# Seven of 22 K-tile pairs of a down projection as Strassen's seven block products

## The chip, the cores and the metric

The kernel runs on one core of one Trainium2 chip. The metric is the device time of one execution in microseconds, from the first to the last instruction and what the launch puts around them; it is given as a median of a few runs. The engines that matter here are TensorE (PE, the matrix multiplier), VectorE (DVE), ScalarE (ACT) and SyncE (SP), whose queue issues the DMAs. Each engine works through its own instructions in the order in which the program lists them and waits on semaphores for the others.

## The reference

One decoder layer on 256 tokens of width 2048, in float32: an input projection, two attention branches that are merged, an output projection, a layer norm, a gated MLP, a second layer norm and a per-layer embedding. The change lies in the MLP and what follows it:

```python
def conv_gated_mlp(x, w_gate, w_up, conv_w, conv_b, w_down):
    g = causal_dwconv(x @ w_gate, conv_w, conv_b)
    h = jax.nn.gelu(g) * (x @ w_up)       # (256, 5632)
    return h @ w_down                     # (256, 5632) @ (5632, 2048)
...
ffn = conv_gated_mlp(x, ...)
x = layer_norm(ALPHA * x + ffn, ln2_g[i], ln2_b[i])
x = x + jax.nn.sigmoid(x @ w_ple_gate[i]) * (p[i] @ w_ple_proj[i])
```

## The kernel before, in words

**Three products for one.** Every operand of a matmul is split into a rounded part `hi` (a ScalarE copy to the type float32r) and a rest `lo` (a VectorE subtraction `raw - hi`). A product is summed from three: hi·hi, hi·lo and lo·hi.

**Units of weights.** All large weights lie in one DRAM array `wu` of units of 128 x 2048 floats (1 MB). `unit()` hands out the next unit and first lets `prep()` (L93) prepare units until two beyond it are under way. For each half of a unit `prep()` issues a DMA into a `raw` buffer (SP, L99), the ScalarE copy to `hi` (L77, in the helper `copy`) and the VectorE subtraction to `lo` (L103). There are four `raw` buffers and six buffers each for `hi` and `lo`, of 128 x 1024 floats; they are reused in rotation, so a new `hi` waits until the matmuls have read the one six places before it.

**Gate and up projection.** For each of 44 tiles `n` of the hidden width (128 channels) the kernel multiplies one unit of `w_gate` and one of `w_up` with all 256 tokens (`gate_up`, L169 and L171), adds the parts (`comb`), applies convolution and GELU, and multiplies. The product `y` (128 channels x 256 tokens) is split into `hi` and `lo` and kept in the list `hT`, the stationary operand of the next stage. This costs one ScalarE copy (L77, `hT<-yc`) and one VectorE subtraction (L989) for each `n`.

**Down projection.** `residual("dn", ...)` calls `x_half` (L227) twice, once for each half `nh` of the 2048 output columns. Each half has four PSUM banks (two token blocks `t` of 128, two column blocks `c` of 512) and goes through 22 units. A unit holds two K tiles of 128 channels by 1024 columns, and costs 24 matmuls of 128x128 by 512 columns (`x_mm`, L213): two K tiles, two token blocks, three products, two column blocks. After the last unit of a half the four banks are added to the residual `z` (L813) and layer norm statistics are taken (L814). In the second half the last two units are kept for a tail which finishes one bank after the other, so that the second layer norm (`ln_out`), its transposes and the projections that follow begin while TensorE still multiplies.

**Order and memory.** The Tile scheduler orders the instructions of TensorE, ScalarE and VectorE, by the program order and by priorities where they are given; the order of SP's DMAs is that of the program. The pool `big` (`s8`) has 15 buffers of 128 x 2048 floats. Activations, residuals and the layer norm's gains share them. PSUM has eight banks: six in the pool `pmm` (`mmtile`) and two in `pmx` (`mxtile`), both used in rotation. In the first half of the down projection, after its unit 4, `mid2` issues the loads of the residual (`z<-x1d`, 2 x 1 MB) and of the gains (`lnb`, 2 x 1 MB).

Of the kernel before, what the change touches and what calls it, by code (L numbers as in the profile page):

```python
# [9 lines left out]
F32 = mybir.dt.float32  # L10
F32R = mybir.dt.float32r
# [23 lines left out]
P_LN1 = (2000, 2000)  # L35
P_LN2 = (4000, 1000)
ZN_DVE = (0,)
AFF_DVE = (0, 2)
# [8 lines left out]
def tile_block(ctx: ExitStack, tc: tile.TileContext, wu, wfv, wpp, xT_in, x_in, pT_in, wlr,  # L47
# [41 lines left out]

    n_prep = [0]  # L90
    ready = {}

    def prep():  # L93
        u = n_prep[0]
        n_prep[0] += 1
        his, los = [], []
        for h in range(2):
            raw = ring.tile([P, 1024], F32, tag="raw", bufs=4, name=f"raw{u}_{h}")
            nc.sync.dma_start(raw, wu[u, :, h * 1024:(h + 1) * 1024])  # L99
            hi = ring.tile([P, 1024], F32R, tag="hi", name=f"hi{u}_{h}")  # L100
            copy(hi, raw)
            lo = ring.tile([P, 1024], F32R, tag="lo", name=f"lo{u}_{h}")
            nc.vector.tensor_tensor(lo, raw, hi.bitcast(F32), ALU.subtract)  # L103
            his.append(hi)
            los.append(lo)
        ready[u] = (his, los)

    n_used = [0]
    NU = wu.shape[0]

# [609 lines left out]

    def ln_out(zs, stats, t, act_out, cg, cb, nm, prio):

        z = zs[t]
        mv = sm.tile([P, 8], F32, tag="mv", name="mv")
# [5 lines left out]
        with tc.high_priority(prio):  # L730
            for g in range(4):
                zc = z[:, g * 512:g * 512 + 512]
                if g in ZN_DVE:
# [83 lines left out]

    def affine(zs, gb_, after, gs=range(4)):
        for t in range(2):
            for g in gs:  # L820
                zc = zs[t][:, g * 512:g * 512 + 512]
                nc.vector.tensor_tensor(zc, zc, gb_[0][:, g * 512:g * 512 + 512], ALU.mult)
                yield
                nc.vector.tensor_tensor(zc, zc, gb_[1][:, g * 512:g * 512 + 512], ALU.add)
                yield
            after(t)
# [45 lines left out]
    def end1(tail_mm):  # L872
# [3 lines left out]
        with tc.manual_schedule(engines={mybir.EngineType.PE}):  # L876
# [59 lines left out]
            for j in range(4):  # L936
                if j < 3:
# [3 lines left out]

    residual("wo", mT, 16, z1, st1, (mid1, lambda: pq.append(ple_prep(0))), end=end1)
    mixers.append(affine(z1, gain[0], lambda t: nc.gpsimd.dma_start(x1d[t], z1[t]),
                         [g for g in range(4) if g not in AFF_DVE]))

# [5 lines left out]
    for i in range(2):  # L951
        nc.gpsimd.memset(gp[i][:, 0:2], 0.0)
    hT = [None] * 11

    def lt(shape, dt, name):
        return late.tile(shape, dt, name=name)

# [8 lines left out]
    for n in range(NF):  # L966
        if n % 4 == 0:
            hT[n // 4] = (s8 if n < 40 else lt)([P, 4, 512], F32R, name=f"hT{n // 4}")
        psg = gate_up(f"psg{n}")
# [15 lines left out]
        comb(psu, u)  # L985
        nc.vector.tensor_tensor(y, y, u, ALU.mult)
        dst = hT[n // 4][:, n % 4, :]
        copy(dst[:, 0:256], y)
        nc.vector.tensor_tensor(dst[:, 256:512], y, dst[:, 0:256].bitcast(F32), ALU.subtract)  # L989
        if n >= 4:  # L990
            pull(1)

    z2 = [s8([P, 2048], name=f"z2{t}") for t in range(2)]
    st2 = [sm.tile([P, 4, 6], F32, tag=f"st2{t}", bufs=1, name=f"st2{t}") for t in range(2)]

    def mid2():
        for t in range(2):
            nc.sync.dma_start(z2[t], x1d[t])
        gain[1] = load_gain(1)

    x2T = [s8([P, 4, 512], F32R, name=f"x2T{g}") for g in range(4)]
    pb, pq = [], []

    def done2(t):
        if t == 1:
            pb.extend(ple_proj(1, *pq[0]))
        ln_out(z2, st2, t, x2T, c_g2, c_b2, "l2", P_LN2[t])

    residual("dn", hT, NF, z2, st2, (mid2, lambda: pq.append(ple_prep(1))), done2)
    pp = [s8([P, 2, 1024], name=f"ppk{i}") for i in range(2)]  # L1010
    for t in range(2):
        for c in range(2):
            copy(pp[1][:, t, c * 512:c * 512 + 512], pb[t][c][0])
    mixers.append(affine(z2, gain[1], lambda t: None))

# [6 lines left out]
    for nh in range(2):  # L1022
        def ev_o(t, c, ps, ab=(0, 512), nh=nh):
            th = t2("tho")
            r = t2("res")
            e = slice(*ab)
            w = slice(c * 512 + ab[0], c * 512 + ab[1])
            o = slice(nh * 1024 + w.start, nh * 1024 + w.stop)
            nc.scalar.activation(th[:, e], ps, AF.Tanh, bias=0.0, scale=0.5)
            nc.vector.scalar_tensor_tensor(th[:, e], th[:, e], 1.0, pp[nh][:, t, w],  # L1030
                                           ALU.add, ALU.mult)
            nc.vector.scalar_tensor_tensor(r[:, e], th[:, e], 0.5, z2[t][:, o],
                                           ALU.mult, ALU.add)
            nc.sync.dma_start(out[t, :, o], r[:, e])
# [15 lines left out]
def _xst(w):  # L1050

    k, n = w.shape
    a = w.reshape(k // 256, 2, P, n // 1024, 1024).transpose(3, 0, 2, 1, 4)
    return a.reshape((k // 256) * (n // 1024), P, 2048)


# [9 lines left out]
def _layout(i):  # L1066
# [4 lines left out]
    for n in range(16):  # L1071
        br.append(bg[n:n + 1])
        if n % 2 == 0:
# [5 lines left out]
         _wst(c("ma", 2048)), _wst(c("mb", 2048))] + br  # L1079
        + [_xst(i["w_out"][0]), gu, _xst(i["w_down"][0]),  # L1080
           _xst(i["w_ple_gate"][0])], 0)
# [43 lines left out]
```

## Time and profile before

| What | Value |
|---|---|
| Median of 3 runs | 1710.17 us (1709.9 to 1710.96) |
| The profiled execution | 1709.5 us |
| Its span, first to last instruction | 1707.6 us |
| PE busy | 1698.3 us (99%) |
| DVE busy, ACT busy | 1098.6 us (64%), 833.4 us (49%) |
| Down projection on the chain that ended last | PE dn L213, 14% of the span |

The page counts an engine as busy while its instructions run; the duration of a matmul overlaps that of the next, so the time of one matmul in a stream is read from the distance of the starts. Times in the trace count from the start of the span. The down projection begins at 1359.2 us, its second half at 1481.5 us, and the tail's transposes (`ptl`) begin at 1601.97 us.

### The profile page before, as it was taken

How to read it: one execution, taken by the hardware profiler on the slowest of the kernel's cores; microseconds unless marked ns; L12 is line 12 of the kernel's file. 1: busy time of each engine (PE TensorE's matmuls, PEld its weight loads, DVE VectorE, ACT ScalarE, POOL GpSimd, SP SyncE). 2: the span in 40 equal slices, each digit the busy share in tenths (PEclk: the TensorE clock that was granted, in tenths of full speed). 3: DMA queues.
4: the chain of work that ended last, by engine and by line, in shares of the span. 5: the costliest groups of instructions: out<-in, count | busy, mean ns of one | idle time of the engine just before them, and what ended most of it. 6: DMA issues, size and time to landing. Idle time of an engine off the chain costs nothing.

```text
span 1707.6 us, 23836 instructions
## 1 busy us (share of the span) xinstructions
PE 1698.3 (99%) x9035; PEld 1455.7 (85%) x9035; DVE 1098.6 (64%) x1588; ACT 833.4 (49%) x1200; POOL 39.3 (2%) x123
## 2 busy tenths in 40 slices
PE   9999999999999999999999999999999999999998
PEld 8888888888888888888788888888888888888787
DVE  6666668758756557774687666666666644544774
ACT  5745445445555544443365445444544533334633
POOL 0000000000000000000010000000000000000000
PEclk9999999999999999999999999999999999999999
DMA  8654455555554555557665555555555575556444
GB/s 310 231 190 166 163 185 173 181 177 172 179 176 165 173 185 189 192 185 281 207 217 195 189 190 187 191 189 186 187 193 187 186 291 189 183 196 197 157 174 171
DMA packets 91427, 330.22 MB, mean 193 GB/s; under 512 B 10232, under 2 KB 11904, under 8 KB 89904
## 3 DMA queue, kind: packets, MB, share of 16 engines
q1 hardware_dynamic: 90528, 324.51, 56.0%
q0 software_dynamic: 784, 4.20, 0.7%
q8 instruction: 70, 1.15, 0.3%
q14 instruction: 45, 0.37, 0.1%
HBM read 323.42 MB, written 5.25 MB: 192 GB/s over the span
## 4 chain that ended last, share of the span: by engine, by line
PE 97%; DVE 1%; DMA 0%; ACT 0%; SPq 0%; issue 0%; POOL 0%
PE dn L213 14%; PE psu L169 9%; PE psg L169 9%; PE psm L169 7%; PE gr L213 5%; PE gv L213 5%; PE wo L213 5%; PE pg L213 5%; PE psu L171 5%; PE psg L171 5%; PE psm L171 4%; PE psa L169 3%; PE fv L320 2%; PE psa L171 2%; PE psfq L169 2%; PE psq L169 2%
## 5 line engine op out<-in xcount | busy, mean ns | idle before, releaser
L103 DVE TENSOR_TENSOR lo<-raw,hi 128x1024 fp32r<-128x1024 f32 x568 | 694.1, 1224 | 520.6 <-ACT hi L77 519.6
L77 ACT ACTIVATE hi<-raw 128x1024 fp32r<-128x1024 f32 x568 | 601.7, 1060 | 745.8 <-issue 275.9
L169 PE MATMUL psu<-x1T,hi 128*128 128x512 f32 x688 | 242.2, 394 | 0.0
L169 PE MATMUL psg<-x1T,hi 128*128 128x512 f32 x672 | 236.5, 393 | 0.0
L213 PE MATMUL dn<-hi,hT 128*128 128x512 f32 x704 | 193.5, 394 | 0.0
L171 PE MATMUL psu<-x1T,lo 128*128 128x256 f32 x688 | 192.6, 280 | 0.0
L171 PE MATMUL psg<-x1T,lo 128*128 128x256 f32 x672 | 188.1, 280 | 0.0
L169 PE MATMUL psm<-xT,hi 128*128 128x512 f32 x512 | 180.1, 395 | 0.0
L213 PEld LDWEIGHTS dn<-hi,hT 128*128 128x128 f32 x704 | 132.1, 188 | 30.6
L169 PEld LDWEIGHTS psu<-x1T,hi 128*128 128x128 f32 x688 | 129.4, 188 | 29.5
L169 PEld LDWEIGHTS psg<-x1T,hi 128*128 128x128 f32 x672 | 126.4, 188 | 28.9
L171 PE MATMUL psm<-xT,lo 128*128 128x256 f32 x512 | 143.3, 280 | 0.0
L171 PEld LDWEIGHTS psu<-x1T,lo 128*128 128x128 f32 x688 | 129.4, 188 | 0.0
L171 PEld LDWEIGHTS psg<-x1T,lo 128*128 128x128 f32 x672 | 126.4, 188 | 0.0
L169 PEld LDWEIGHTS psm<-xT,hi 128*128 128x128 f32 x512 | 96.2, 188 | 21.6
L213 PE MATMUL dn<-lo,hT 128*128 128x512 f32 x352 | 111.3, 393 | 0.0
L171 PEld LDWEIGHTS psm<-xT,lo 128*128 128x128 f32 x512 | 96.5, 188 | 0.2
L169 PE MATMUL psa<-oT,hi 128*128 128x512 f32 x256 | 90.1, 393 | 0.0
L213 PEld LDWEIGHTS dn<-lo,hT 128*128 128x128 f32 x352 | 66.1, 188 | 15.7
L213 PE MATMUL gv<-hi,xT 128*128 128x512 f32 x256 | 73.6, 399 | 0.0
L213 PE MATMUL gr<-hi,xT 128*128 128x512 f32 x256 | 73.5, 399 | 0.0
L213 PE MATMUL wo<-hi,mT 128*128 128x512 f32 x256 | 71.8, 395 | 0.0
(248 smaller groups left out, 2438.8 us busy)
## 6 DMA issues: line engine op xcount, KB each, us to landing
raw<-in_wu_dram SPq DMA_DIRECT2D x568, 512.0 KB, 3.6
fvraw<-in_wfv_dram SPq DMA_DIRECT2D x14, 524.0 KB, 6.3
lnb<-in_lng_dram SPq DMA_DIRECT2D x4, 1024.0 KB, 12.4
z<-in_x_dram SPq DMA_DIRECT2D x2, 1024.0 KB, 9.6
praw<-in_wpp_dram SPq DMA_DIRECT2D x4, 512.0 KB, 4.8
x1d<-z POOLq DMA_DIRECT2D x2, 1024.0 KB, 4.4
z<-x1d SPq DMA_DIRECT2D x2, 1024.0 KB, 7.6
xraw<-in_xT_dram SPq DMA_DIRECT2D x7, 256.0 KB, 6.5
```

The lines of the kernel that those rows point to most:

```text
L77: nc.scalar.activation(o, i, AF.Copy, bias=0.0, scale=scale)
L103: nc.vector.tensor_tensor(lo, raw, hi.bitcast(F32), ALU.subtract)
L169: nc.tensor.matmul(ps, lhsT=hi[i // 8 if hoff == 0 else 0][:, w0 % 1024:w0 % 1024 + P], rhs=a[:, kt % 4, :], start=first and i == 0, stop= ...
L171: nc.tensor.matmul(ps[:, 256:512], lhsT=lo[i // 8 if hoff == 0 else 0][:, w0 % 1024:w0 % 1024 + P], rhs=a[:, kt % 4, 0:256], start=False, ...
L213: nc.tensor.matmul(bs[j][:, 0:m], lhsT=x, rhs=v[:, o:o + m], start=first and i == 0, stop=last and i == 2)
L320: nc.tensor.matmul(fbk[t][c][:, 0:n], lhsT=x, rhs=w[:, o:o + n], start=kt == 0 and i == 0, stop=kt == 15 and i == 2)
```

## The change

Write a pair of K tiles as a product of 2 x 2 blocks: the activations as blocks of 128 tokens by 128 channels, the weights as blocks of 128 channels by 512 columns. The plain product needs eight block products, Strassen's (in Winograd's form) seven. The three float32r products for each block product stay. Of the 22 pairs, seven (`DN_S`) are multiplied so, in both halves: 21 matmuls for a unit in place of 24.

Left operands: for each of these pairs `sums()` makes four sums and differences of activation blocks (VectorE), and splits seven blocks into `hi` and `lo`. For the pairs 1, 4 and 7 this follows their `n`; for the pairs 10, 13, 16 and 19 (`DN_Y`) `y` is kept unsplit in a buffer `hY`, and `sums()` stands after the loop over `n`.

Right operands: `prep_s()` takes the place of `prep()` for these units, in both halves. It makes four differences T1 to T4 of weight blocks (VectorE) and splits seven blocks in six pieces: b21 and b22 together as one half unit of 1024 columns, and b11 and T1 to T4 one by one, 512 columns each. It takes six `hi` and six `lo` buffers, where a plain unit takes two of each.

The products go to seven PSUM banks: three are banks of the plain result, four (p1, p5, p6, p7) are new and are summed over all seven pairs. After the last such pair `fold()` adds them to the residual `z2` (one ScalarE copy, eight VectorE operations for each half). The plain result is added at the end of the half as before, with an add in place of a multiply-add. The units come in the order `DN_ORDER` (plain C, Strassen S): C S C C S C S C C S C S C C S C S C C C C C. The weights are laid out for this on the host.

Loads: the residual is loaded by halves (2 x 512 KB each), after unit 8 of the first half and after unit 6 of the second; the gains after unit 11 of the second half. The per-layer embedding's preparation (`ple_prep(1)`) stays after unit 17 of the second half.

```diff
+DN_S = (1, 4, 7, 10, 13, 16, 19)
+DN_Y = (10, 13, 16, 19)
+DN_ORDER = (0, 1, 2, 3, 4, 5, 7, 6, 8, 10, 9, 13, 11, 12, 16, 14, 19, 15, 17, 18, 20, 21)
...
+    def split512(src, name):
+        hi = ring.tile([P, 512], F32R, tag="hi", name=f"{name}h")
+        copy(hi, src)
+        lo = ring.tile([P, 512], F32R, tag="lo", name=f"{name}l")
+        nc.vector.tensor_tensor(lo, src, hi.bitcast(F32), ALU.subtract)
+        return hi, lo
+
+    def prep_s(u):
+        r0, r1 = [ring.tile([P, 1024], F32, tag="raw", bufs=4, name=f"raw{u}_{h}")
+                  for h in range(2)]
+        for h, r in enumerate((r0, r1)):
+            nc.sync.dma_start(r, wu[u, :, h * 1024:(h + 1) * 1024])
+        b12, b11, b22, b21 = r0[:, 0:512], r0[:, 512:1024], r1[:, 0:512], r1[:, 512:1024]
+        ops = [split512(b11, f"b11_{u}")]
+        hi = ring.tile([P, 1024], F32R, tag="hi", name=f"hi{u}_1")
+        copy(hi, r1)
+        lo = ring.tile([P, 1024], F32R, tag="lo", name=f"lo{u}_1")
+        nc.vector.tensor_tensor(lo, r1, hi.bitcast(F32), ALU.subtract)
+        ops += [(hi[:, 512:1024], lo[:, 512:1024]), (hi[:, 0:512], lo[:, 0:512])]
+        ts = {}
+        for n, a, b in (("T1", b12, b11), ("T3", b12, b22), ("T2", b22, "T1"),
+                        ("T4", b21, "T2")):
+            ts[n] = t2(f"{n}_{u}")
+            nc.vector.tensor_tensor(ts[n], a, ts.get(b, b) if isinstance(b, str) else b,
+                                    ALU.subtract)
+        for n in ("T1", "T3", "T2", "T4"):
+            ops.append(split512(ts[n], f"{n}_{u}"))
+        ready[u] = ops
...
+    def sums(y, pair):
+        a11, a21, a12, a22 = [y[:, k, t * P:t * P + P] for k in range(2) for t in range(2)]
+        v = t2("sums").rearrange("p (i t) -> p i t", t=P)
+        o = hS[pair] = s8([P, 7, 256], F32R, name=f"hS{pair}")
+        for i, a, b, op in ((0, a21, a22, ALU.add), (2, a21, a11, ALU.subtract),
+                            (1, v[:, 0], a11, ALU.subtract), (3, a12, v[:, 1], ALU.subtract)):
+            nc.vector.tensor_tensor(v[:, i], a, b, op)
+        for e, src in ((slice(0, 1), y[:, 0:1, 0:P]),
+                       (slice(1, 3), y[:, 1, :].rearrange("p (t n) -> p t n", t=2)),
+                       (slice(3, 7), v)):
+            copy(o[:, e, 0:P], src)
+            nc.vector.tensor_tensor(o[:, e, P:256], src, o[:, e, 0:P].bitcast(F32),
+                                    ALU.subtract)
...
+        prods = (p1, C[0][0], C[0][1], p5, p7, p6, C[1][0])
...
+        def strassen(pair, ops):
+            for ps, i, (hi, lo) in zip(prods, left, ops):
+                ah, al = hS[pair][:, i, 0:P], hS[pair][:, i, P:256]
+                for x, v in ((ah, hi), (ah, lo), (al, hi)):
+                    mm(ps, x, v)
+
+        def fold():
+            g0, g1 = 2 * nh, 2 * nh + 1
+            u = t2("fold")
+            copy(u, p1)
+            axpy(z2of(0, g0), p1)
+            add(u, p6)
+            axpy(z2of(0, g1), u)
+            add(z2of(0, g1), p5)
+            add(u, p7)
+            axpy(z2of(1, g0), u)
+            add(u, p5)
+            axpy(z2of(1, g1), u)
...
+        for i, pair in enumerate(DN_ORDER[:n - tail]):
+            (strassen if pair in DN_S else classic)(pair, unit())
+            if i in mid:
+                mid[i]()
+            if pair == DN_S[-1]:
+                fold()
...
+    down(0, 0, {8: lambda: load_z2(0)})
+    down(1, 2, {6: lambda: load_z2(1), 11: late_loads, 17: lambda: pq.append(ple_prep(1))})
```

135 lines of the change are left out of this document (107 added, 28 removed).

## The prediction

> **What bounds the kernel now.** I read the page first: engine shares, then the chain that ended last.
>
> ```profile
> span 1707.6 us, 23836 instructions
> PE 1698.3 (99%) x9035; PEld 1455.7 (85%) x9035; DVE 1098.6 (64%) x1588; ACT 833.4 (49%) x1200; POOL 39.3 (2%) x123
> ...
> PE 97%; DVE 1%; DMA 0%; ACT 0%; SPq 0%; issue 0%; POOL 0%
> ...
> L213 PE MATMUL dn<-hi,hT 128*128 128x512 f32 x704 | 193.5, 394 | 0.0
> ...
> L213 PE MATMUL dn<-lo,hT 128*128 128x512 f32 x352 | 111.3, 393 | 0.0
> ```
>
> TensorE is the bound: 97% of the chain, and in the down projection (704 + 352 = 1056 matmuls) it never sits idle. A matmul less shortens the run, as long as the operands come in time. What one costs is in the table by stretches (PE busy, weight loads, clock, DMA share, GB/s; L213 alone), its first row being the first half:
>
> ```profile
> 1359.20:1481.50 122.30, 122.17 (x528) 99.12 (x529) 1.00 0.64 223
> 1481.50:1598.60 117.10, 117.10 (x507) 94.87 (x506) 1.00 0.61 200
> ```
>
> 528 matmuls in 122.3 us are 0.2316 us each. A plain unit (24) takes 5.56 us, a Strassen unit (21) 4.86 us.
>
> The operands come from a loop over ScalarE, VectorE and the DMA queue. Its rows in the timeline, from the first to the second half:
>
> ```profile
> 1472.15 0.42 PEld L213 LDWEIGHTS dn<-lo,hT 128*128 128x128 f32 x2
> 1473.52 1.06 ACT L77 ACTIVATE hi<-raw 128x1024 fp32r<-128x1024 f32 x1 [1.73 <-PE dn L213]
> 1474.61 1.23 DVE L103 TENSOR_TENSOR lo<-raw,hi 128x1024 fp32r<-128x1024 f32 x1 [1.56 <-ACT hi L77]
> 1481.33 2.47 DVE L813 SCALAR_TENSOR_TENSOR z<-z,dn 128x512 f32<-128x512 f32 x4
> 1486.10 3.62 DVE L103 TENSOR_TENSOR lo<-raw,hi 128x1024 fp32r<-128x1024 f32 x3
> ```
>
> ScalarE waits for TensorE to give up a `hi` buffer (1.73 us), VectorE for ScalarE (1.56 us). Both have slack. The last two rows give the distance of operations that follow each other: (2.47 - 0.68) / 3 = 0.60 us for 512 columns, (3.62 - 1.23) / 2 = 1.20 for 1024. Alone they last, by the groups of this stage:
>
> ```profile
> L103 DVE TENSOR_TENSOR lo<-raw,hi 128x1024 fp32r<-128x1024 f32 x87 | 106.4, 1225 | 122.7 <-ACT hi L77 122.5
> L752 DVE TENSOR_TENSOR x2T<-lny,x2T 128x512 fp32r<-128x512 f32 x2 | 1.4, 687 | 0.0
> L989 DVE TENSOR_TENSOR hT<-yc,hT 128x256 fp32r<-128x256 f32 x1 | 0.4, 418 | 0.0
> L77 ACT ACTIVATE hi<-raw 128x1024 fp32r<-128x1024 f32 x89 | 94.5, 1061 | 141.1 <-PE dn L213 127.5 <-DMA raw<-in_wu_dram 8.3 <-issue 3.0
> L77 ACT ACTIVATE x2T<-lny 128x512 fp32r<-128x512 f32 x2 | 1.3, 626 | 0.0
> L77 ACT ACTIVATE hT<-yc 128x256 fp32r<-128x256 f32 x1 | 0.4, 400 | 0.0
> ```
>
> **The change, part by part.**
>
> *Matmuls removed.* 7 pairs x 2 halves x 3 = 42, so 42 x 0.2316 = 9.73 us, all of it on TensorE's path. They keep their shape and one weight load each. A Strassen product puts three in a row into one bank, where a plain unit alternates between two; the gate and up stage puts 32 in a row into one, and two neighbouring starts of its 512-column matmuls, with one of 256 columns between, are 0.35 us apart, which is 0.23 + 0.12:
>
> ```profile
> 1357.57 0.40 PE L169 MATMUL psu<-x1T,hi 128*128 128x512 f32 x1
> 1357.80 0.28 PE L171 MATMUL psu<-x1T,lo 128*128 128x256 f32 x1
> 1357.92 0.40 PE L169 MATMUL psu<-x1T,hi 128*128 128x512 f32 x1
> ```
>
> So no charge for that. The Trainium skill ("TensorE: Matmul & The Clock Gate", section Back-to-back issue gap) gives N/2.4 + 2.5 ns for an isolated gap, 216 ns here, and about 131 ns in a sustained stream. By these, as an estimate, the gain would be 9.07 or 5.50 us. The measured 231.6 ns disagrees with both, and it decides.
>
> *Weights of a Strassen unit.* VectorE: four differences and five `lo` parts of 512 columns and one of 1024: 9 x 0.687 + 1.225 = 7.41 us (back to back 9 x 0.60 + 1.20 = 6.6), against 2 x 1.225 = 2.45 for a plain unit. ScalarE: 5 x 0.626 + 1.061 = 4.19 us against 2.12. A Strassen unit's 4.86 us do not cover 7.41; a Strassen and a plain unit together need 9.86 us on VectorE against 10.42 on TensorE. In the order given, units 1 to 16 are seven Strassen and nine plain: 7 x 7.41 + 9 x 2.45 = 73.9 us of VectorE in 7 x 4.86 + 9 x 5.56 = 84.1 of TensorE, 88%. It fits on average; what decides is whether it fits in time, since a Strassen unit takes all six buffers and its last `hi` cannot be written before the plain unit ahead of it has ended.
>
> The next numbers come from walking the built program's order of the four engines by hand through its tightest places, with the durations above and the landing times below. Time 0 is the first matmul of the stage; units 1, 2, 4, 5 start at 5.56, 10.42, 21.54 and 26.40.
> - Unit 2 (plain, after the first Strassen unit). Unit 1's half unit is split at -3.0 (its buffer is free at -5.55, then 1.06 and 1.225, and 0.3 of waits). From there VectorE's list up to the last late sum (below) holds 31 operations, 13.7 us alone, about 11.5 back to back, with some 1.3 of waits for ScalarE: it ends between 9.8 and 10.7, unit 2's first `lo` 1.2 later, at 11.0 to 11.9. TensorE wants that two matmuls into the unit, at 10.88: 0.1 to 1.0 us of wait.
> - Units 4 to 6 (S C S). VectorE's order puts the next Strassen unit's T1, T3, T2 and T4 before the `lo` of T4 of this one, and T3 waits for a raw buffer that is free only after this unit's T4 (19.2). With 3.6 to 4.5 us to land that is 22.8 to 23.7, three differences end at 24.8 to 25.7, the `lo` at 25.4 to 26.4. TensorE wants it at 21.54 + 19 x 0.2316 = 25.94: 0 to 0.4 us. Unit 5's first `lo` follows at 26.6 to 27.6 and is wanted at 26.86: up to 0.7 in all.
> - The other two blocks (units 9 to 11 and 14 to 16) come out 1 to 3 us ahead; in the second half units 1 and 4 come about 2 us earlier, for no sums stand before them.
>
> Together 0.1 to 1.7 us in the first half, 0 to 0.3 in the second. I take 0.6, nearer the low end, since the rows show operations that follow each other overlapping.
>
> *Activations.* For each of the seven pairs VectorE gets four operations of 128 columns and `lo` parts of 128, 256 and 512, with the price of 128 columns from another stage:
>
> ```profile
> L573 DVE TENSOR_TENSOR kq<-gq,e 128x128 f32<-128x128 f32 x56 | 13.7, 285 | 0.0
> ```
>
> 5 x 0.285 + 0.418 + 0.687 = 2.53 us in place of 2 x 0.418. For pairs 1, 4 and 7 that is 1.7 us more in two steps of the gate and up stage, which has room (columns PE, PEld, DVE, ACT, POOL):
>
> ```profile
> 1100.00:1200.00 100.00, 100.00 (x575) 87.70 (x574) 68.26 (x99) 49.36 (x72) 3.12 (x17) 1.00 0.56 190
> ```
>
> 31.7 us of 100 are free on VectorE: no cost. The other four pairs, 10.1 us, stand at the end of that stage, because their buffers are those of `x1T` and `hS10` to `hS19` are written as the last unit lets go of them; ScalarE's copies for unit 1 wait behind them. That is the wait at unit 2 above.
>
> *Fold and ends.* Eight VectorE operations of 0.69 and one ScalarE copy of 0.63 in each half, after unit 16, beside five plain units (27.8 us of TensorE, 12.3 of VectorE): hidden, also with `ple_prep` (2 x 1.225 + 2 x 0.418 = 3.3 us) in the second half, after which the tail's last `lo` is about 0.5 us early. At the change of halves the new half begins in the two banks of p7 and p6, and needs the first half's banks six matmuls later; the four adds start as before. The tail's order on TensorE is the same.
>
> *Loads.* How they behave when large ones come first is in the page's DMA issues, the same for 1365 to 1420 us, the timelines of SP and of ACT, and a stretch of 4 us (its last number is GB/s):
>
> ```profile
> raw<-in_wu_dram SPq DMA_DIRECT2D x568, 512.0 KB, 3.6
> ```
> ```profile
> raw<-in_wu_dram SPq DMA_DIRECT2D x20, 512.0 KB, 4.5
> ```
> ```profile
> 1373.48 0.84 SPq L998 DMA_DIRECT2D z<-x1d  x2
> 1374.38 1.36 SPq L831 DMA_DIRECT2D lnb<-in_lng_dram  x2
> 1375.84 22.53 SPq L99 DMA_DIRECT2D raw<-in_wu_dram  x9
> ```
> ```profile
> 1388.86 1.06 ACT L77 ACTIVATE hi<-raw 128x1024 fp32r<-128x1024 f32 x1 [6.02 <-DMA raw<-in_wu_dram]
> 1380.00:1384.00 4.00, 4.00 (x19) 3.25 (x18) 2.36 (x2) 1.13 (x2) 0.00 (x0) 1.00 1.01 424
> ```
>
> The median landing is 3.6 us over the run and 4.5 between 1365 and 1420. There 4 MB went before a raw tile at 424 GB/s; ScalarE sat 6.02 us and TensorE not at all. After the change the loads come as 1, 1 and 2 MB: 2.5, 2.5 and 5 us at that rate. SP is past them before it asks for the next Strassen unit's tiles (the gains are asked for near 57 us after a half's start, unit 14's first tile at 61.5, wanted by 65.3). In the second half their buffers were last read in its units 1, 2 and 4, so SP does not wait. Taken as 0; without that cover up to 2 us.
>
> **Sum.** 1709.5 of the profiled execution (span 1707.6) is 0.67 under the median 1710.17; counted from the median, 1710.17 - 9.73 + 0.6 = 1701.0 us.
>
> **The rivals.**
>
> *Partial waits.* The same gain, but landing times or waits between engines cost more than in my walk. If raw tiles land 1 us later, each of the six S C S blocks loses 0.7 us, and unit 2 of the first half 1.0 (above): 6 x 0.7 + 1.0 = 5.2 us of wait, 1710.17 - 9.73 + 5.2 = 1705.6; half of it gives 1703. For it: 88% load with six buffers. Against it: VectorE today waits for ScalarE 1.56 us in every half unit.
>
> *VectorE becomes the bound (slower).* If a Strassen unit's preparation cannot run ahead, because its unit takes all six buffers, each shows 7.41 - 4.86 = 2.55 us: 14 x 2.55 = 35.7, so 1710.17 - 9.73 + 35.7 = 1736. It decides from 9.73 / 14 = 0.70 us a unit. Against it: the four differences need no ring buffer, and four of the six buffers come free during the plain units ahead.
>
> *The clock falls.* If TensorE's pauses let its clock fall, matmuls would take twice as long, as in the first microseconds of the run (a `lo` matmul after three in 0.88 us, later in 0.48):
>
> ```profile
> 5.30 0.49 PE L320 MATMUL fv<-fvlo,xT 128*128 128x352 f32 x1
> 6.18 0.49 PE L320 MATMUL fv<-fvlo,xT 128*128 128x352 f32 x1
> ...
> 9.21 0.32 PE L320 MATMUL fv<-fvlo,xT 128*128 128x352 f32 x1
> 9.69 0.32 PE L320 MATMUL fv<-fvlo,xT 128*128 128x352 f32 x1
> ```
>
> All 14 x 21 = 294 Strassen matmuls at double time are 68 us more, 1769; 42 of them undo the gain. A rule of the Trainium skill says so for this pattern ("TensorE: Matmul & The Clock Gate", section A second HAM failure mode: psum-queue depth-cycling): going through PSUM banks in each iteration left small pauses between groups of matmuls, and the clock swung. Against it: a pause of 1.66 us before the second layer's inputs left the next matmuls at full pace, and mine are shorter.
>
> ```profile
> 872.23 0.39 PE L182 MATMUL psg<-x1T,hi 128*128 128x256 f32 x1 [1.66 <-DVE x1T L801]
> 872.45 0.28 PE L186 MATMUL psg<-x1T,lo 128*128 128x256 f32 x1
> ```
>
> **How the numbers follow.** Forecast (0 to 2 us of wait, 1700.4 to 1702.4) 0.60; partial waits 0.20, of which 0.02 end within 0.2%; VectorE as the bound 0.17, of which 0.04 end within 0.2% and 0.13 above; clock 0.03, slower. A measurement here can tell about 0.2% (3.4 us) from no change. Faster 0.60 + 0.18 = 0.78, same 0.06, slower 0.16. The range runs from no wait at all less half a microsecond of scatter, 1699.9, to the end of the partial waits plus as much, 1706.1; it leaves out 0.2. The forecast alone: 1699.9 to 1702.9.
>
> **What would show it.** 1014 matmuls of `dn` in place of 1056 at 0.23 us; TensorE busy from the stage's first matmul to the tail but for waits of tenths near units 2, 4 and 5; VectorE near 88% busy in units 1 to 16; ScalarE's idle time before `hi` still put down to TensorE. Wrong would be TensorE idle before Strassen units with the `lo` of T4 or T2 as releaser, raw tiles that land later than 4.5 us, or matmuls further apart than 0.2316.

## The result, and the profile after

The changed kernel takes 1708.16 us (median of 20 runs, 1703.66 to 1711.19), the kernel before, beside it, 1710.14 (20 runs, 1708.91 to 1712.17): a ratio of 0.9986, with a 95% interval of 0.9979 to 0.9992. The forecast was 1701.0, with a range to 1706.1. Some 2 us of the 9.73 remain. The interval lies below 1, but the gain is smaller than the 0.2% that the prediction took as the least that can be told from no change. The runs lie 7.5 us apart where those of before lie 3.3 apart.

The profiled execution took 1707.28 us (before 1709.5). Its page, with span, engines and the shares of the chain that ended last:

```profile
span 1705.4 us, 24004 instructions
PE 1691.5 (99%) x8993; PEld 1447.4 (85%) x8993; DVE 1174.7 (69%) x1751; ACT 862.5 (51%) x1265; POOL 39.4 (2%) x123
...
PE 93%; DVE 3%; DMA 2%; ACT 1%; issue 1%; SPq 0%; POOL 0%; ACTq 0%; DVEq 0%
```

TensorE has 42 matmuls less (9035 before), as meant. But its part of the chain fell from 97 to 93%: VectorE and DMA now stand on the path. The busy share of 99% does not show it, for slow matmuls count as busy too.

The stage shows where. These are TensorE's rows at the start of the stage, at the start of the second half's tail (the row at 1585.04 holds the last two matmuls before the tail and the tail's first) and around the tail's transposes (start, duration, instruction, idle time before it and its releaser):

```profile
1359.44 0.63 PE L1106 MATMUL dn<-hi,hC 128*128 128x512 f32 x2
...
1585.04 0.86 PE L1106 MATMUL dn<-hi,hC 128*128 128x512 f32 x3
...
1593.74 0.40 PE L1106 MATMUL dn<-hi,hC 128*128 128x512 f32 x1
1597.28 1.09 PE L780 MATMUL ptl<-ident,z 128*128 128x128 f32 x8 [3.14 <-DVE z L774]
...
1598.85 1.05 PE L1106 MATMUL dn<-hi,hC 128*128 128x512 f32 x2
1599.70 0.63 PE L1106 MATMUL dn<-lo,hC 128*128 128x512 f32 x1
...
1602.99 0.39 PE L254 MATMUL pp<-pw,pTs 128*128 128x512 f32 x1
```

In the kernel before, the first matmul of the stage, the tail's first transposes and the first matmul of the next projection are

```profile
1359.33 0.63 PE L213 MATMUL dn<-hi,hT 128*128 128x512 f32 x2
...
1601.97 1.09 PE L740 MATMUL ptl<-ident,z 128*128 128x128 f32 x8 [0.55 <-DVE z L734]
...
1606.14 1.79 PE L213 MATMUL pp<-pw,pTs 128*128 128x512 f32 x7
```

From first row to last the stage took 246.81 us before and 243.55 after: 3.26 us gained of 9.73. The missing 6.47 are

| Loss | us | How it is worked out |
|---|---|---|
| Lost before the tail | 2.34 | 1585.04 - 1359.44 = 225.60, less 964 matmuls x 0.2316 = 223.26 |
| Pause before the transposes | 2.59 | 3.14, against 0.55 before |
| Slow matmuls behind the pause | 1.71 | granted clock, next fence |
| Rest | -0.17 | 6.47 less the rows above; the pace of 0.2316 is rounded |

Not all of the first row are waits: the kernel with the plain split (below), which shows no wait at the places named below, loses 0.63 us by the same count (1585.05 - 1361.16 = 223.89). That leaves 1.71 us of waits.

About 1 us more was lost after the stage (3.26 gained there, 2.2 in the whole execution). 0.72 us of it lie behind the last matmul, which starts 5.27 us before the end of the span, against 4.55 in the kernel before; the cause was not pursued.

After the pause two neighbouring matmuls stand (1599.70 - 1598.85) / 2 = 0.43 us apart, not 0.23. Stretches of the same execution show why (columns as in the prediction; the third number from the end is the granted clock):

```profile
1598.00:1599.00 1.00, 1.00 (x7) 0.85 (x6) 1.00 (x3) 1.00 (x3) 0.00 (x0) 0.73 0.00 0
1599.00:1601.00 2.00, 2.00 (x7) 1.52 (x6) 1.65 (x4) 1.82 (x5) 0.00 (x0) 0.50 0.00 0
1601.00:1602.00 1.00, 1.00 (x4) 0.81 (x3) 1.00 (x2) 1.00 (x3) 0.00 (x0) 0.56 0.00 0
```

The clock goes to 0.50 and comes back: 0.27 + 2 x 0.50 + 0.44 = 1.71 us lost, so 3.42 us at half speed.

Why the pause? VectorE's timeline in the tail:

```profile
1590.18 2.57 DVE L146 TENSOR_TENSOR lo<-raw,hi 128x1024 fp32r<-128x1024 f32 x2 [2.39 <-ACT hi L83]
1592.67 0.68 DVE L1144 TENSOR_TENSOR z<-z,dn 128x512 f32<-128x512 f32 x1
```

and ScalarE's:

```profile
1589.08 1.06 ACT L83 ACTIVATE hi<-raw 128x1024 fp32r<-128x1024 f32 x1 [2.55 <-DMA raw<-in_wu_dram]
```

The two `lo` at 1590.18 belong to the first unit of the *next* stage. VectorE's written order has them ahead of the first evacuation `z<-z,dn`. They wait 2.39 us for a `hi`, which waits for its raw tile, and the evacuation waits behind them, though its bank had been complete since about 1588.6 (the tail's twelfth matmul starts at 1588.18 and takes 0.40 us). The order is not new. In the kernel before, too, the two `lo` of the next stage's first unit (the second of them at 1594.17) stand ahead of the first evacuation. But there they come in time, and the evacuation waits for TensorE:

```profile
1594.17 1.23 DVE L103 TENSOR_TENSOR lo<-raw,hi 128x1024 fp32r<-128x1024 f32 x1 [1.57 <-ACT hi L77]
1595.87 0.69 DVE L813 SCALAR_TENSOR_TENSOR z<-z,dn 128x512 f32<-128x512 f32 x1 [0.48 <-PE dn L213]
```

What the change added is the delay. The chain of waits says why the raw tile is late: of 1564.86 to 1592, its two longest pieces are loads into a raw buffer which VectorE had just let go of, with the fold's and `ple_prep`'s operations in between:

```profile
1567.69 1.23 DVE lo L146
1568.94 5.25 DMA raw<-in_wu_dram
...
1580.60 0.68 DVE fold L1131
...
1582.55 2.28 DVE lo L146 x2
1584.85 5.47 DMA raw<-in_wu_dram
```

The waits before the tail are at the S C S places. TensorE's weight loads at two of them, in the first half (units 4 and 5, and unit 14; the first `lo` of unit 15 follows with 0.37 us at 1440.22):

```profile
1385.65 0.19 PEld L1106 LDWEIGHTS dn<-T_228l,hS 128*128 128x128 f32 x1 [0.46 <-DVE T_228l L107]
1386.79 0.30 PEld L1106 LDWEIGHTS dn<-lo,hC 128*128 128x128 f32 x2 [0.36 <-DVE lo L146]
1439.09 0.19 PEld L1106 LDWEIGHTS dn<-T_238l,hS 128*128 128x128 f32 x1 [0.44 <-DVE T_238l L107]
```

The second half has such rows at its units 5, 9, 10 and 15, of 0.28 to 0.44 us. VectorE at the first place:

```profile
1382.98 0.69 DVE L127 TENSOR_TENSOR T<-raw,raw 128x512 f32<-128x512 f32 x1 [1.18 <-DMA raw<-in_wu_dram]
1383.59 1.41 DVE L127 TENSOR_TENSOR T<-raw,T 128x512 f32<-128x512 f32 x2
1384.92 0.69 DVE L107 TENSOR_TENSOR T_228l<-T,T_228h 128x512 fp32r<-128x512 f32 x1
```

Three differences of the next Strassen unit, the first of them waiting for a load, stand ahead of the `lo` that TensorE wants now.

### The profile page after: what moved, and what is told of

Same layout as the page of the kernel before. It is cut to its first block, busy times and chain, and to the rows that moved or that the text cites. A ratio compares the mean times of both kernels' runs of the same rounds, so it can differ in the third digit from the quotient of the medians.

```text
span 1705.4 us, 24004 instructions
## 1 busy us (share of the span) xinstructions
PE 1691.5 (99%) x8993; PEld 1447.4 (85%) x8993; DVE 1174.7 (69%) x1751; ACT 862.5 (51%) x1265; POOL 39.4 (2%) x123
## 3 DMA queue, kind: packets, MB, share of 16 engines
HBM read 323.42 MB, written 5.25 MB: 193 GB/s over the span
## 4 chain that ended last, share of the span: by engine, by line
PE 93%; DVE 3%; DMA 2%; ACT 1%; issue 1%; SPq 0%; POOL 0%; ACTq 0%; DVEq 0%
PE dn L1106 10%; PE psu L210 9%; PE psg L210 9%; PE psm L210 7%; PE gr L254 5%; PE gv L254 5%; PE psu L212 5%; PE psg L212 5%; PE pg L254 4%; PE psm L212 4%; PE psa L210 3%; PE wo L254 3%; PE fv L361 2%; PE dn_p L1106 2%; DMA raw<-in_wu_dram 2%; PE psa L212 2%
## 5 line engine op out<-in xcount | busy, mean ns | idle before, releaser
L146 DVE TENSOR_TENSOR lo<-raw,hi 128x1024 fp32r<-128x1024 f32 x540 | 658.1, 1223 | 407.0 <-ACT hi L83 405.8
L83 ACT ACTIVATE hi<-raw 128x1024 fp32r<-128x1024 f32 x554 | 585.6, 1059 | 644.4 <-issue 253.2
L1106 PE MATMUL dn<-hi,hC 128*128 128x512 f32 x480 | 135.8, 397 | 0.0
L1106 PEld LDWEIGHTS dn<-hi,hC 128*128 128x128 f32 x480 | 90.9, 189 | 21.5
L1106 PE MATMUL dn<-lo,hC 128*128 128x512 f32 x240 | 77.8, 400 | 0.0
L212 PE MATMUL psa<-oT,lo 128*128 128x256 f32 x256 | 71.6, 280 | 0.0
```

The costliest lines, as they stand in the source:

```text
L83: nc.scalar.activation(o, i, AF.Copy, bias=0.0, scale=scale)
L212: nc.tensor.matmul(ps[:, 256:512], lhsT=lo[i // 8 if hoff == 0 else 0][:, w0 % 1024:w0 % 1024 + P], rhs=a[:, kt % 4, 0:256], start=False, ...
L1106: nc.tensor.matmul(ps, lhsT=x, rhs=w, start=todo[id(ps)] == total[id(ps)], stop=todo[id(ps)] == 1)
```

## The experiments

Medians of the kernels below are beside the kernel before on the same chip: 1709.97 us in the first group of four, 1709.70 in the second, 1709.55 with the pauses. A difference from the changed kernel is one between medians of different groups, and the kernel before differs by up to 0.44 us between them (1710.14 beside the changed kernel).

### The tail's order on VectorE

The next stage's two units are prepared after the tail's first normalisation; a copy of one column from the normalised `z` into the `lo` buffer holds the order on VectorE, whatever the scheduler would prefer.

```diff
-    def prep():
+    def prep(gate=None):
...
+            if gate is not None:
+                nc.vector.tensor_copy(lo[:, 0:1], gate)
             nc.vector.tensor_tensor(lo, raw, hi.bitcast(F32), ALU.subtract)
...
-        while n_prep[0] < min(NU, u + 3):
+        while n_prep[0] < min(NU, u + 3, lim):
...
             if tail:
                 done2(t)
+                if t == 0:
+                    for _ in range(2):
+                        prep(z2of(0, 0)[:, 0:1])
```

> The two units of the next stage are prepared after the first tail units' evacuations on VectorE, not ahead of them; everything else is as in the changed kernel. Theory A (VectorE stands at a late tile of the next stage while TensorE has long finished the first bank, TensorE then pauses 3.1 us and its clock falls for some 4 us): the first evacuation starts near 1588.5 instead of 1592.7, the pause before the transposes goes from 3.14 to under 1 us, the matmuls behind it stand 0.23 us apart instead of 0.43, the time falls by 2.5 + 2.0 us to about 1703.5, and the runs lie closer together than 7 us. Rival B (the clock falls because of the order in which the Strassen products go through the banks, not because of the pause): the pause goes, the scatter of the runs and the slow matmuls stay, 1705 to 1706. Rival C (the loads are the bound, the wait only moves): the pause reappears before the next stage's matmuls, 1707 to 1708.

Measured: 1704.63 us (6 runs, 1703.47 to 1708.27), ratio 0.9971 [0.9960, 0.9983]. The tail:

```profile
1599.32 1.10 PE L782 MATMUL ptl<-ident,z 128*128 128x128 f32 x8 [0.56 <-DVE z L776]
...
1600.49 0.40 PE L1108 MATMUL dn<-lo,hC 128*128 128x512 f32 x1
1600.72 0.62 PE L1108 MATMUL dn<-hi,hC 128*128 128x512 f32 x2
```

The pause is back at the 0.56 us of before, the matmuls behind it stand 0.23 us apart: 3.5 us less than the changed kernel. Theory A holds for the tail. The scatter, 4.8 us over six runs, is under the 7 us of the expectation, but wider than the 2.8 of the kernel before beside it. The profiled execution was the slowest of its six (1708.27); it had a fall of the clock too, but near the start of the program, long before the change:

```profile
10.00:20.00 10.00, 7.61 (x36) 7.04 (x36) 6.90 (x7) 6.98 (x8) 0.00 (x0) 0.83 0.92 330
```

In the same execution TensorE waited 1.38 us in unit 15 of the second half, at 1563.13, where the changed kernel's weight load had waited 0.37: VectorE had stood 1.81 us for a raw tile just before (until 1561.25).

### T4's `lo` first

```diff
             ts[n] = t2(f"{n}_{u}")
+            if n in ("T3", "T2") and tok:
+                nc.vector.tensor_copy(ts[n][:, 0:1], tok[0])
...
             ops.append(split512(ts[n], f"{n}_{u}"))
+        tok[:] = [sm.tile([P, 1], F32, tag="tok", name="tok")]
+        nc.vector.tensor_copy(tok[0], ops[-1][1][:, 0:1].bitcast(F32))
```

> In a Strassen unit VectorE makes the next Strassen unit's T3, T2 and T4 only after the lo part of this one's T4; three copies of one column a unit hold the order. Theory A (the order of VectorE's list, not its load, makes the waits at the S C S places): the waits on T4's lo and on the following plain unit's first lo (0.44 and 0.37 us each place, 1.9 us in all until the tail) go, the tail stays as it is: 1 to 1.8 us less than the changed kernel in a run with the same tail. Rival B (VectorE is simply too loaded there, or the raw tiles land too late): the waits move to the T parts of the next Strassen unit, the sum of waits stays at 1.5 us or more, the time within 0.5 us of the changed kernel or above.

Measured: 1705.96 us (8 runs, 1704.79 to 1708.14), 0.9977 [0.9967, 0.9987], 2.2 us less than the changed kernel. VectorE and TensorE's weight loads at the place shown above:

```profile
1381.15 0.69 DVE L108 TENSOR_TENSOR T_228l<-T,T_228h 128x512 fp32r<-128x512 f32 x1 [0.81 <-ACT T_228h L83]
1381.87 0.15 DVE L135 COPY tok<-T_228l 128x1 f32<-128x1 f32 x1
...
1382.25 0.69 DVE L130 TENSOR_TENSOR T<-raw,raw 128x512 f32<-128x512 f32 x1
```
```profile
1384.42 0.19 PEld L1111 LDWEIGHTS dn<-T_228l,hS 128*128 128x128 f32 x1
```

The `lo` of T4 now starts at 1381.15 and is read at 1384.42 without a wait; before the tail one wait of a weight load over 0.25 us was left (0.67). So at this place the order made the wait, not the load. The trace shows it; the time alone would not, for the two intervals (0.9967 to 0.9987, and 0.9979 to 0.9992 for the changed kernel) overlap. The tail stayed as it was, with a pause of 3.00 us, and its fall of the clock lasted twice as long as in the changed kernel's profile:

```profile
1594.00:1595.00 1.00, 0.00 (x0) 0.00 (x0) 0.37 (x2) 0.12 (x1) 0.56 (x1) 0.78 0.30 123
1595.00:1601.00 6.00, 5.65 (x18) 4.79 (x19) 4.35 (x9) 4.76 (x9) 0.00 (x0) 0.50 0.01 3
1601.00:1602.00 1.00, 1.00 (x8) 0.81 (x6) 0.33 (x2) 1.00 (x2) 0.00 (x0) 0.81 0.12 25
```

That is 0.44 + 6 + 0.38 = 6.82 us at half speed.

### Both edits

The two diffs above together.

> Both edits, the tail's order and T4's lo first. Theory A: the sum of both gains, about 1702 us, 1701 to 1703, close to the 1701.0 of the prediction; the rest is some 0.9 us in the next stage. Rival (loads are the bound): no better than the better of the two alone.

Measured: 1702.46 us (5 runs, 1701.84 to 1704.71), 0.9959 [0.9946, 0.9973]: 5.7 us less than the changed kernel, faster than both kernels of the case (the interval is clear of the changed kernel's), and 1.5 above the 1701.0 forecast.

```profile
1359.19 0.63 PE L1113 MATMUL dn<-hi,hC 128*128 128x512 f32 x2
...
1592.92 1.09 PE L787 MATMUL ptl<-ident,z 128*128 128x128 f32 x8 [0.54 <-DVE z L781]
...
1597.09 1.09 PE L261 MATMUL pp<-pw,pTs 128*128 128x512 f32 x4
```

The stage takes 237.90 us, 8.91 less than before. VectorE does all the change asks of it, plus the small copies; only the order differs. The span is 7.4 us shorter than before (1700.2 against 1707.6), so 1.5 of the 8.91 are lost behind the stage: 0.72 behind the last matmul, as in the changed kernel, and the rest in the next stage, where a weight load waits 0.70 us at 1602.09 and another 0.54 at 1661.84.

### The transposes later

```diff
                 nc.vector.bn_stats(st2[t][:, g, :], z2of(t, g))
+                if (nh, t, c) == (1, 0, 1):
+                    for _ in range(2):
+                        nc.vector.tensor_scalar(z2of(0, 3), z2of(0, 3), 1.0, None, ALU.mult)
+                    nc.vector.bn_stats(st2[0][:, 3, :], z2of(0, 3))
```

> VectorE gets three operations of 512 columns more (two multiplications by 1 and a repeated statistic) between the second evacuation and the means, some 1.9 us, nothing is taken away; the written order of TensorE then has the last 12 matmuls of the down projection and 8 of the next ones ahead of the first transposes, in place of behind them. Theory A (a pause in TensorE is what costs, once by its length and once by the clock behind it; what VectorE does later is hidden): the evacuation is as late as before, 1592.7, the first transposes come 2 us later than in the changed kernel, but TensorE has 4.6 us of matmuls to fill the time: no pause over 1 us, matmuls 0.23 us apart throughout, about 1703 us, although VectorE does more. Rival (VectorE's delay itself sets the end of the stage): slower than the changed kernel, 1709 to 1710.

Measured: 1706.35 us (10 runs, 1704.46 to 1707.97), 0.9978 [0.9969, 0.9987]. Neither theory had it right.

```profile
1599.84 0.13 DVE L767 TENSOR_SCALAR mv<-mv 128x1 f32<-128x1 f32 x1
1599.89 1.21 DVE L146 TENSOR_TENSOR lo<-raw,hi 128x1024 fp32r<-128x1024 f32 x1
1601.56 0.21 DVE L769 TENSOR_SCALAR mv<-mv 128x1 f32<-128x1 f32 x1 [0.46 <-POOL mv L768]
```

The added work changed the order once more: other operations, among them a `lo` of 1.21 us, came between the steps of the means. The transposes waited 2.65 us after all and the clock fell behind them for 3.42 us. The experiment was confounded and decides nothing between the theories. Its median lies 1.8 us under the changed kernel's although it only adds work and its profile still has the pause, so a difference of that size between two single edits proves little.

### What makes VectorE late: the fold, the next projection's weights, the differences

Three more take one load away each. First, the second half's fold is left out:

> The fold of the second half is left out: the four product banks of that half are not added into the result (eight operations of 512 columns less on VectorE and one copy on ScalarE, 4.8 us back to back on VectorE, all of them in the five units before the end of the stage); the rest is the changed kernel. Theory A (the fold beside the preparation of the last units and of the next projection is what makes VectorE late in the tail): the tile of the next stage that stands ahead of the first evacuation is ready some 3 us earlier, the pause before the transposes goes from 3.14 to under 1 us, the clock stays at 1.00 there, 1704 to 1705; the waits at the S C S places stay. Rival B (the last units' raw tiles land late whatever VectorE does): pause and time as in the changed kernel, 1707 to 1708.

```diff
-            if pair == DN_S[-1]:
+            if pair == DN_S[-1] and nh == 0:
                 fold()
```

Measured: 1705.06 us (10 runs, 1703.39 to 1707.96), 0.9972 [0.9962, 0.9981], 3.1 us less. The profiled execution (1707.03, 2 us above the median) still has a pause of 2.17 us and a fall of 3.41 us at half speed. Theory A was near in the time and wrong on the pause: as far as this one profile shows, the fold is a part of the cause, not all of it.

Then `ple_prep` after unit 8 in place of 17:

> The preparation of the next projection's weights is issued after unit 8 of the second half instead of after unit 17; nothing else is edited. Theory A: 3.3 us of VectorE's work and 1 MB and more of loads leave the last five units, the pause before the transposes shrinks from 3.14 to 0.5 to 1 us, the clock holds, 1704 to 1705; the units 9 to 11 may wait 0.5 us longer for their parts. Rival B (the fold alone suffices, or the place does not matter): the pause stays over 2 us, 1707 to 1708. Rival C (the loads wait for buffers and hold up the queue): waits of over 1 us near unit 9 or 10 of the second half, 1708 or more.

```diff
-    down(1, 2, {6: lambda: load_z2(1), 11: late_loads, 17: lambda: pq.append(ple_prep(1))})
+    down(1, 2, {6: lambda: load_z2(1), 11: late_loads, 8: lambda: pq.append(ple_prep(1))})
```

Measured: 1705.86 us (11 runs, 1704.40 to 1708.10), 0.9977 [0.9968, 0.9986].

```profile
1554.89 0.49 PE L1106 MATMUL dn<-hi,hS 128*128 128x512 f32 x1 [0.50 <-ACT hi L83]
1556.15 0.50 PE L1106 MATMUL dn<-lo,hS 128*128 128x512 f32 x1 [0.76 <-DVE lo L121]
...
1596.78 1.09 PE L780 MATMUL ptl<-ident,z 128*128 128x128 f32 x8 [0.55 <-DVE z L774]
```

The pause is gone, as theory A has it, and new waits stand at unit 14 of that half: the load moved into that block. With this edit beside the two on the order (the three diffs above together) the same happens:

> The tail's order, T4's lo first, and the preparation of the next projection after unit 8 of the second half. Theory A: the two waits of 0.34 us that were left in the down projection go too, 1701.5 to 1702.5, no slow matmuls. Rival (the loads of the projection collide with those of units 9 to 11): a new wait of 0.5 us or more there, 1702.5 to 1704.

Measured: 1706.02 us (9 runs, 1703.62 to 1707.00), 0.9975 [0.9965, 0.9986], 3.6 us worse than the two order edits without it. The rival's waits came, and the time lies above its 1704. TensorE waits 0.90 and 0.23 us in unit 9, 0.48 and 0.76 in unit 14. For unit 14 ScalarE waits for a raw tile:

```profile
1552.78 0.63 ACT L83 ACTIVATE b_260h<-raw 128x512 fp32r<-128x512 f32 x1 [5.19 <-DMA raw<-in_wu_dram]
```

The wait itself is not new: in the changed kernel ScalarE stands 5.22 us for the same tile, up to 1548.88, since the 2 MB of gains were asked for just before it (at 1535.27). There the tile comes 4.4 us before its unit begins (1553.28). Here the projection's loads hold up the queue, the gains are asked for at 1539.51, and the tile comes 1.0 us before (1553.80). So place 17 was the better one, once the order behind it is right.

Last, the Strassen units split as plain ones: T1 to T4 are not made, so VectorE has 2 x 1.2 us a unit, while TensorE's matmuls keep their number, shapes and banks.

```diff
-        ops = [split512(b11, f"b11_{u}")]
...
+        sp = []
+        for h, r in enumerate((r0, r1)):
...
+            sp += [(hi[:, c:c + 512], lo[:, c:c + 512]) for c in (0, 512)]
+        ops = [sp[k] for k in (1, 0, 1, 2, 3, 2, 3)]
```

> The Strassen units are split as plain ones: the differences T1 to T4 are not made, and the products multiply slices of the two plain halves instead (the matmuls keep their number, shapes, order and banks; the products are then not Strassen's). VectorE makes 2 x 1.2 us a unit in place of 6.6. Theory A (the waits inside the stage come from the Strassen units' preparation, those in the tail from the fold, the next projection and the order): the 1.9 us of waits at the S C S places go, the tail's pause stays over 2 us, 1705 to 1707. Rival B (the banks' order slows the matmuls themselves): matmuls 0.2316 us apart no longer hold, the time stays at 1707 to 1708. Rival C (the load of the differences is also behind the tail's pause): pause under 1 us, 1701.5 to 1703.

Measured: 1700.85 us (5 runs, 1700.72 to 1703.03), 0.9951 [0.9938, 0.9964]. Rival C held, not theory A: with the differences gone the tail's pause is gone too (0.55 us), fold and `ple_prep` notwithstanding, and the time lies just under its 1701.5. This is what the fewer matmuls bring when their operands come in time: 1709.70 - 1700.85 = 8.85 us. The edit does not part VectorE's work from the buffers, for a unit split so also takes two `hi` and two `lo` buffers in place of six. It also clears the banks: the same sequence of banks, the same threes in a row, and no slow matmul in the stage.

### Pauses in the kernel before

To see whether the clock falls without any Strassen product, one `lo` part in each of four plain units of the kernel before is multiplied by 1 on VectorE a given number of times:

```diff
             nc.vector.tensor_tensor(lo, raw, hi.bitcast(F32), ALU.subtract)
+            if h == 0:
+                for _ in range(PAUSE.get(u - (NU - 16 - NF), 0)):
+                    nc.vector.tensor_scalar(lo, lo.bitcast(F32), 1.0, None, ALU.mult)
```

> The kernel before the change, with four units of the down projection (6 and 16 of the first half, 6 and 14 of the second) whose first lo part is multiplied by 1 on VectorE 10, 11, 12 and 13 times, so that TensorE stands at four places of growing length; no Strassen product, no other bank order. By the rows (a lo part is ready some 8 us ahead, one multiplication of 1024 columns is estimated at 0.95 us) the pauses would be about 1, 2, 3 and 4 us. Theory A (the pause makes the clock fall, with plain matmuls too): behind the pauses of about 3 us and more the granted clock shows 0.50 for some microseconds and neighbouring matmuls stand 0.43 us apart, behind the shortest they stay at 0.23; 1709.5 plus the pauses plus 2 to 4 us for each fall. Rival (the fall belongs to the Strassen kernel's banks or to the transposes): 1.00 behind all four.

Measured: 1712.5 us (one run). Two pauses came out as none, the others as 0.47 and 2.15 us, and the clock is 1.00 behind both; nothing to tell the theories apart. Hence two kernels with longer ones:

> As the kernel with four pauses, with 16 and 17 multiplications in units 6 and 16 of the first half and 16 and 15 in units 6 and 14 of the second. There 12 and 13 in the second half gave pauses of 0.47 and 2.15 us with the clock at 1.00, and one multiplication takes 0.72 us: about 3.4 us (0.47 + 4 x 0.72) and 3.6 us (2.15 + 2 x 0.72) in the second half, 2 to 5 in the first. Theory A (a pause of 2.2 to 3.6 us can make the clock fall whatever the matmuls are): granted clock 0.50 for 3 to 7 us behind most of the pauses over 2.5 us. Rival (the fall needs the Strassen kernel): 1.00 behind all four.

> The same with 14 and 15 multiplications in units 6 and 16 of the first half and 14 and 14 in units 6 and 14 of the second: about 1.9 us (0.47 + 2 x 0.72) and 2.9 us (2.15 + 0.72) in the second half. Theory A: no fall behind pauses up to 2.2 us (2.15 us left the clock at 1.00), a fall behind some of those from 2.5 us. If a pause of under 2 us is followed by 0.50, length alone does not decide, and where the pause lies in time does too.

Measured: 1735.22 and 1722.94 us (one run each). Where the clock changes at the first fall, in the first of them (the granted clock of 1 us):

```profile
1397.00:1398.00 1.00, 1.00 (x5) 0.82 (x4) 1.00 (x2) 0.00 (x0) 0.00 (x0) 0.72 0.60 221
1400.00:1401.00 1.00, 1.00 (x4) 0.79 (x3) 0.22 (x1) 0.74 (x1) 0.00 (x0) 0.58 0.96 266
```

A clock of 0.72 in one microsecond is 0.56 us at 0.50, so the first fall begins at 1397.44; a clock of 0.58 is 0.84 us, so it ends at 1400.84. The stretch between is at 0.50. In this way (the pause of 0.47 us and those that came out as none are left out):

| Kernel | Pause (us) | From, to | Half speed from, to | Length |
|---|---|---|---|---|
| pauses | 2.15 | 1561.00, 1563.15 | none | |
| pauses_long | 2.26 | 1394.31, 1396.57 | 1397.44, 1400.84 | 3.40 |
| pauses_long | 5.11 | 1454.04, 1459.15 | 1458.88, 1462.28 | 3.40 |
| pauses_long | 4.39 | 1527.56, 1531.95 | 1530.56, 1537.38 | 6.82 |
| pauses_long | 3.61 | 1579.21, 1582.82 | 1581.76, 1588.58 | 6.82 |
| pauses_mid | 3.66 | 1449.00, 1452.66 | 1452.52, 1455.92 | 3.40 |
| pauses_mid | 2.93 | 1521.14, 1524.07 | 1524.20, 1527.60 | 3.40 |
| pauses_mid | 2.89 | 1570.40, 1573.29 | none | |

TensorE's rows behind the shortest pause with a fall, in `pauses_long`, and behind the longest without one, in `pauses_mid`:

```profile
1396.57 0.73 PE L217 MATMUL dn<-lo,hT 128*128 128x512 f32 x2 [2.26 <-DVE lo L107]
```
```profile
1573.29 0.73 PE L217 MATMUL dn<-lo,hT 128*128 128x512 f32 x2 [2.89 <-DVE lo L107]
```

Theory A holds: plain matmuls fall to half speed as well. Length alone does not decide, though: 2.26 us was enough, 2.89 was not.

## Why the prediction was wrong

The forecast missed by 7.2 us; the rival nearest to the outcome is *partial waits*. It has the waits at the S C S places, but neither the tail's pause nor the clock, and its upper end (1705.6) is still 2.6 us too low. Its steps:

- *Matmuls removed* (9.73): right in mechanism and nearly in size. With VectorE's extra work taken away 8.85 us are left, and the stage itself (237.62 us with the plain split, 246.81 before) gives 9.19. Three products in a row into one bank cost nothing, as argued.
- *Weights of a Strassen unit* (0.6 of wait): the mechanism was right, the size was not. At units 4 and 5 of the first half T4's `lo` began at 1384.92 and ended about 26.2 us into the stage, inside the 25.4 to 26.4 of the walk, and the waits stand where it put them. But I took the other two blocks of a half to be 1 to 3 us ahead, and the second half to be nearly free. In fact units 14 and 15, and 5, 9, 10 and 15 of the second half, wait in the same way, since the same order of VectorE's list repeats at each S C S. Measured 2.34 us lost before the tail, 1.71 of them waits: three times the value I took, and nearly half of it in the second half, where I had allowed 0.3. That 1.71 lies inside the bounds of both halves together (0.1 to 2.0) is luck, for unit 2 of the first half, with 0.1 to 1.0 foreseen, shows no wait.
- *Activations*: right, no cost: the stage begins at 1359.44, 0.11 us later than before.
- *Fold and ends* (0): the step that failed most. I counted VectorE's operations against TensorE's time (12.3 us of `lo`, 5.5 of fold, 3.3 of `ple_prep` in 27.8) and concluded "hidden", with the tail's last `lo` 0.5 us early. That last `lo` was indeed only some 0.3 us late. What I did not look at is the next entry in VectorE's list: two `lo` of the next stage, ahead of the first evacuation, as in the kernel before. By the chain of waits, each operation between a `lo` and its successor delays the release of a raw buffer and so the next load; that loop came out 2.4 us late at an entry with the evacuation queued behind it. "The tail's order on TensorE is the same" was true and beside the point. Price: 2.59 us of pause.
- *Loads* (0): SP is not past the gains before the next Strassen unit's tile matters: unit 14's first tile of the second half came 5.22 us after ScalarE was ready for it. TensorE did not wait in unit 14, so the charge of 0 held there; whether the waits at unit 15 come from it is open. In the tail the loop of four raw buffers carried the delay: 5.25 and 5.47 us from a release to the next tile, against the 3.6 and 4.5 us of landing that I used (the median from 1560 to 1592 was 5.3, and 4.8 in the kernel before).
- *The clock falls* (chance 0.03): "mine are shorter" was wrong: the tail's pause was 3.14 us, not under 1.66. Nor is 1.66 us safe as such (last section). The price was 1.71 us in the profiled execution and 3.41 in another, not 68: it is paid once for each pause, not once for each matmul. Cycling through the banks, the pattern named beside it, was not the cause: the plain split has the same banks in the same order, and the clock stays at 1.00 in the whole stage.

Why the runs of the changed kernel lie 7.5 us apart is shown in part. Pauses of 2 to 5 us cost nothing, 1.7 or 3.4 us of clock according to when they fall, and in two of the profiled executions (tail order, plain split) a fall near the program's start cost about 1.7 us. How late the raw tiles come differs too (the 1.38 us at unit 15 above); how much of the scatter is due to each is argued.

## What to carry to other kernels

An engine with room on average can still hold the bottleneck up: look in the built order for what stands directly ahead of each operation that the bottleneck waits for, and ask when *its* input arrives. Here two edits that only reorder, with a copy of one column as a fence that the scheduler must keep, brought 5.7 us where dropping the second fold or moving `ple_prep` brought 3.1 and 2.3. (Only the 5.7, and the plain split, have intervals clear of the changed kernel's.) A pause of TensorE should be priced at its length plus the clock behind it: here a fall could follow from 1.6 us of idle time in one step of the next section, and did each time from 2.17 on.

## What the runs showed of the hardware

The falls of the clock lie on a grid. In the kernel with long pauses they begin at 1397.44, 1458.88, 1530.56 and 1581.76: distances of 61.44, 71.68 and 51.20 us, which are 18.00, 21.00 and 15.00 times 3.413. They last 3.40 or 6.82 us, one or two steps. With the steps drawn on the time axis, a fall follows each step in which TensorE was idle for 2.17 us or more (2.17 in the kernel without the second fold, 2.26 in the step 1394.03 to 1397.44). The pause of 2.89 us is divided by the step's end at 1571.98 (1524.20 + 14 x 3.413) into 1.58 and 1.31, and nothing falls. The clock comes back at the first step's end if TensorE was busy for nearly all of that step (idle 0 to 0.27 us), and only one step later if it had been idle in it for 0.79 us (`t4_first`), 1.06 or 1.39 (the two of 6.82). The pauses of the Strassen kernels fit: 2.23 us idle in the step before 1598.46 in the changed kernel, 2.21 before 1594.56 with T4's `lo` first.

Below 2.17 us the idle time of a step does not decide alone. Here is one step with a fall behind it, with the tail's order, and one without, in the kernel without the second fold (behind the step's length stands TensorE's busy time):

```profile
11.58:15.00 3.42, 1.82 (x10) 1.54 (x11) 2.36 (x3) 2.79 (x4) 0.00 (x0) 1.00 1.00 399
```
```profile
870.19:873.60 3.41, 1.76 (x16) 1.52 (x15) 3.41 (x7) 1.57 (x3) 0.00 (x0) 1.00 0.98 309
```

The first, near the start of the program, has about 1.6 us of idle time, and the clock is at 0.50 from 15.00 to 18.41. The second has 1.65, and the clock stays at 1.00. The fall near the start with the plain split follows a step with 1.70 us. What else counts, no run shows.

The Trainium skill ("TensorE: Matmul & The Clock Gate", section What's actually happening) states this step: a window of 3413 ns that runs freely, with half speed after an idle window. The trace agrees on the window: 3.413 us. On what counts as idle it differs. The Trainium skill's section "HAM oscillation — how this bites in real kernels" on the same page gives as the rule no pause over some 3.4 us; here 2.17 and 2.26 us sufficed, and the measurement decides.
